# Splitting every weight chunk on VectorE, with ten pairs of places in the second part of a two-layer decoder trunk

## The chip, the core and the metric

The kernel runs on one core of a Trainium2 chip. The core has five engines that each work through their own list of instructions in order: TensorE (PE; its weight loads are shown apart as PEld), VectorE (DVE), ScalarE (ACT), GpSimd (POOL) and SyncE (SP, which here only issues DMA transfers). They wait for each other by semaphores. The metric is the device time of one execution in microseconds; lower is better.

## The reference

Two decoder layers over 256 tokens of width 1024, in float32. Cut to what matters here:

```python
for layer in range(2):
    h = rwkv_moba_mixer(x, ...) if layer == 0 else dilated_mixer(x, c_w_in, c_w_out, pos)
    x = layer_norm(2 ** 0.5 * x + h, ln1_g[layer], ln1_b[layer])
    m = square(relu(x @ mlp_w1[layer])) @ mlp_w2[layer]        # 1024 -> 4096 -> 1024
    x = layer_norm(2 ** 0.5 * x + m, ln2_g[layer], ln2_b[layer])

# the mixer of layer 0: z = x @ ab_w_in; eight RWKV-7 heads and four block-attention heads; y @ ab_w_out
# the mixer of layer 1: z = x @ c_w_in;  24 query heads in three window groups over 8 key/value heads; o @ c_w_out
```

## The kernel before

**The weights are one stream of 211 chunks** of 128x1024 float32 (512 KB each), in the order in which they are used: 0 to 26 for the projections of layer 0, 27 to 34 for its output projection, 35 to 98 for the MLP of layer 0, 99 to 102 for half of the values of layer 1, 103 to 134 for its queries and keys (four chunks a head), 135 to 138 for the other values, 139 to 146 for its output projection, 147 to 210 for the MLP of layer 1. A transfer brings each into one of the `raw` tiles (four in the first part, six in the second); SyncE issues it when the chunk that lay there before has been split.

**Splitting.** From chunk 17 on a chunk isn't multiplied as it is. ScalarE writes `hi`, the chunk rounded to the fast matmul type (L95), and then another engine writes `lo`, the rest: `lo = raw - hi` (L97). The activations are split alike (`xh` and `xl`, `yh` and `yl`, `hh` and `hl`; L240 on ScalarE and L241 on VectorE), and each product takes three matmuls: high by high, low by high and high by low. `Stream.split` decides who writes `lo`: VectorE, or GpSimd for the chunks that the tuple `ON_POOL` names. These are 34 (the end of the output projection of layer 0), 36 to 39 and 42 (the first chunks of the MLP of layer 0), 100, and 150, 151, 161, 164 and 169 (MLP of layer 1).

**Places.** A split chunk lies in a pair of places (`hi`, `lo`) of a ring. The ring has four pairs (`NW1`) until the output projection of layer 0, when `add_pairs` puts `NW2` more in front. From there on `cur["np"]` is the number of pairs and `cur["look"]` is that less two: when the matmuls of chunk i are written, the split of chunk i + look is written ahead of them. It takes the place of chunk i - 2, so ScalarE can write it as soon as TensorE is done with that one.

**The transitions.** `tail` runs the last chunks of a matrix product, first for the token half 0, then for the half 1. The layer norm of half 0 (class `LN`; L260 and L261 sum and take statistics, L271 to L273 the reciprocal root, with a power on GpSimd at L273, L285 and L286 apply it) is computed on VectorE while TensorE multiplies for half 1; TensorE then transposes the normed half (L297) into `xh` and `xl`, and `by_token` starts the next product with half 0 while VectorE norms half 1. In `rest`, `up` computes four more groups of the MLP with the weights stationary (L225), and `up_trans` brings the first group into the same layout (L388, L240, L241). The rotary embedding of layer 1 (`rope`) uses VectorE (L859, L862) and GpSimd (L861, L863).

**Order.** The code is written in program order; a scheduler with priorities turns it into one list for each engine, and so may put an instruction earlier or later than it is written. `tc.high_priority()` pulls the layer norm forward. The three transitions that the prediction speaks of are: the output projection of layer 0 into its MLP (about 166 to 212 us), that MLP into layer 1 (about 356 to 383 us), and the output projection of layer 1 into its MLP (about 532 to 580 us).

Of the kernel before, what the change touches and what calls it, by code (L numbers as in the profile page):

```python
# [37 lines left out]
NCHUNK = 211  # L38

UNSPLIT = 17  # L40
ON_POOL = (34, 36, 37, 38, 39, 42, 100, 150, 151, 161, 164, 169)


STATIONARY = [1] * 9 + [0] * 4 + [1] * 14 + [0] * 8
_MLP = [0] * 8 + [1] * 8 + [0] * 16 + ([1] * 8 + [0] * 8) * 2
STATIONARY += _MLP + [0] * 4 + [1] * 32 + [0] * 12 + _MLP
LINE, STAT_AT = 64, 56
NW1, NW2, NR, NR2 = 4, 4, 4, 2
NS4, NS2 = 13, 6
RIGHT = "right"  # L50
HS = 8 * (16 * P + 16)
# [75 lines left out]
def trunk(ctx: ExitStack, tc: tile.TileContext, w_all, x_nat, x_t, par_in, lora_in, gup2_in, ln_in,  # L127
# [80 lines left out]
    st.load(1 + NR)  # L208
    st.on_pool = set(ON_POOL)

# [1106 lines left out]
```

## Time and profile before

| | |
|---|---|
| runs | 742.39, 736.24 and 742.59 us; median 742.39 us |
| profiled execution | 736.11 us, of which its span is 734.0 us |
| PE busy | 702.7 us (96%) |
| DVE busy | 477.6 us (65%) |
| ACT busy | 333.8 us (45%) |
| POOL busy | 154.9 us (21%) |
| granted TensorE clock, mean | 0.977 |

Busy time counts an instruction from its start to its end, also while it is held up in between; so a row that takes longer than its like elsewhere is a sign of something beside it. PE's figure has little room in it, and what matters is where its 31 us of idle time and its stretches at a lower clock lie. The clock is given as a share of full speed: 1.00 stands for 2.4 GHz and 0.50 for 1.2 GHz.

### The profile page before, as it was taken

The numbers are of one execution on the slowest core, as the hardware profiler recorded it, in microseconds if no ns is written. First come the engines' busy times: TensorE is split into PE (matmuls) and PEld (weight loads), VectorE is DVE, ScalarE is ACT, GpSimd is POOL, SyncE is SP. The second block draws the span as 40 slices with busy tenths as digits, with TensorE's granted clock in tenths as the row PEclk, the third lists the DMA queues.
The fourth block names the chain that finished last, engine by engine and source line by source line (L and its number), as shares of the span: only waits on it lengthen the run. The fifth ranks groups of instructions, "written<-read, shape, count | busy, mean of one in ns | idle before, by whom it ended". The sixth has DMA issues, their size and how long they took to land. (4 is left out here: it accounts for less than half of the span.)

```text
span 734.0 us, 11556 instructions
## 1 busy us (share of the span) xinstructions
PE 702.7 (96%) x4572; PEld 626.6 (85%) x4572; DVE 477.6 (65%) x733; ACT 333.8 (45%) x485; POOL 154.9 (21%) x115
## 2 busy tenths in 40 slices
PE   8999989998999999999999899999999999999995
PEld 6867888996789889989879799997878898998985
DVE  3748983579786545546598767885497754464645
ACT  4712446253375435545155445554436453363520
POOL 3000032026200000000014867785131110000001
PEclk9999995999899999999999999999999999999998
DMA  8366362037674666565088533443537565655401
GB/s 308 130 188 187 118 179 78 29 128 275 200 260 147 204 194 199 183 199 192 31 286 295 165 116 118 142 152 107 174 106 254 168 211 184 198 197 175 144 1 58
DMA packets 40566, 122.61 MB, mean 167 GB/s; under 512 B 8128, under 2 KB 10816, under 8 KB 40384
## 3 DMA queue, kind: packets, MB, share of 16 engines
q1 hardware_dynamic: 37856, 119.94, 49.5%
q10 hardware_dynamic: 2656, 1.93, 0.9%
q8 instruction: 36, 0.59, 0.3%
q14 instruction: 18, 0.15, 0.1%
HBM read 119.49 MB, written 2.36 MB: 166 GB/s over the span
## 5 line engine op out<-in xcount | busy, mean ns | idle before, releaser
L97 DVE TENSOR_TENSOR lo<-raw,hi 128x1024 fp32r<-128x1024 f32 x182 | 237.7, 1310 | 137.0 <-ACT hi L95 135.3
L95 ACT CAST hi<-raw 128x1024 fp32r<-128x1024 f32 x194 | 202.1, 1049 | 198.3 <-PE bank L231 98.2
L225 PE MATMUL bank<-xh,hi 128*128 128x256 f32 x720 | 175.7, 284 | 0.0
L225 PE MATMUL bank<-xl,hi 128*128 128x256 f32 x720 | 173.8, 281 | 0.0
L225 PEld LDWEIGHTS bank<-xh,hi 128*128 128x128 f32 x720 | 136.2, 189 | 1.4 <-issue 0.7
L225 PEld LDWEIGHTS bank<-xl,hi 128*128 128x128 f32 x720 | 136.4, 189 | 0.5
L231 PE MATMUL bank<-hi,hl 128*128 128x512 f32 (+1 forms) x288 | 105.8, 368 | 1.9 <-DVE hl L241 1.9
L232 PE MATMUL bank<-lo,hh 128*128 128x512 f32 (+1 forms) x288 | 105.3, 366 | 0.0
L230 PE MATMUL bank<-hi,hh 128*128 128x512 f32 (+1 forms) x288 | 104.7, 367 | 0.3 <-ACT hh L240 0.3
L225 PE MATMUL bank<-xh,lo 128*128 128x256 f32 x720 | 100.3, 281 | 0.0
L225 PEld LDWEIGHTS bank<-xh,lo 128*128 128x128 f32 x720 | 91.5, 190 | 0.0
L273 POOL TENSOR_TENSOR rs<-rs,mhalf 128x1 f32<-128x1 f32 x8 | 7.7, 960 | 321.4 <-DVE rs L272 321.4
L861 POOL TENSOR_TENSOR qk<-qk,ropec 32x512 f32<-32x512 f32 x20 | 49.9, 2496 | 79.2 <-DVE sw L859 79.2
L231 PEld LDWEIGHTS bank<-hi,hl 128*128 128x128 f32 x288 | 54.3, 189 | 11.1 <-DVE hl L241 2.5
L230 PEld LDWEIGHTS bank<-hi,hh 128*128 128x128 f32 x288 | 54.2, 189 | 9.5 <-ACT hh L240 0.5
L232 PEld LDWEIGHTS bank<-lo,hh 128*128 128x128 f32 x288 | 54.2, 188 | 8.8
L217 PE MATMUL bank<-xst,raw 128*128 128x256 f32 x208 | 46.2, 381 | 1.2 <-DMA xst<-in_x_t_dram 1.2
L217 PEld LDWEIGHTS bank<-xst,raw 128*128 128x128 f32 x208 | 39.2, 190 | 8.3 <-DMA xst<-in_x_t_dram 2.4
L97 POOL TENSOR_TENSOR lo<-raw,hi 128x1024 fp32r<-128x1024 f32 x12 | 30.3, 2533 | 56.2 <-ACT hi L95 50.5
L232 PE MATMUL bank<-lo,xh 128*128 128x512 f32 x96 | 37.7, 393 | 0.6 <-DVE lo L97 0.5
L230 PE MATMUL bank<-hi,xh 128*128 128x512 f32 x96 | 38.1, 396 | 0.0
L231 PE MATMUL bank<-hi,xl 128*128 128x512 f32 x96 | 37.5, 391 | 0.1
(236 smaller groups left out, 896.5 us busy)
## 6 DMA issues: line engine op xcount, KB each, us to landing
raw<-in_w_all_dram SPq DMA_DIRECT2D x210, 512.0 KB, 3.5
g<-in_ln_dram SPq DMA_DIRECT2D x4, 512.0 KB, 5.5
b<-in_ln_dram SPq DMA_DIRECT2D x4, 512.0 KB, 6.2
dA<-abT ACTq DMA_DIRECT2D x2, 512.0 KB, 3.6
x<-in_x_nat_dram SPq DMA_DIRECT2D x1, 1024.0 KB, 4.8
dmask<-in_dmask_dram SPq DMA_DIRECT2D x1, 576.0 KB, 6.5
xst<-in_x_t_dram ACTq DMA_DIRECT2D x2, 256.0 KB, 5.6
xst<-in_x_t_dram SPq DMA_DIRECT2D x2, 256.0 KB, 5.7
```

Source lines behind the costliest of these rows:

```text
L95: self.nc.scalar.copy(hi[:, cols], r[:, cols])
L97: eng.tensor_tensor(lo[:, cols], r[:, cols], hi[:, cols].bitcast(F32), ALU.subtract)
L217: nc.tensor.matmul(ps, hl[:, k * P:(k + 1) * P], xraw(k), start=k == 0, stop=k == KT - 1)
L225: nc.tensor.matmul(ps, w[:, k * P:(k + 1) * P], a[:, k, :], start=n == 0, stop=n == 3 * KT - 1)
L230: nc.tensor.matmul(acc, ah, hi[:, cols], start=first, stop=False)
L231: nc.tensor.matmul(acc, al, hi[:, cols], start=False, stop=False)
L232: nc.tensor.matmul(acc, ah, lo[:, cols], start=False, stop=last)
L273: nc.gpsimd.tensor_tensor(rs, rs, mhalf, ALU.pow)
L861: nc.gpsimd.tensor_tensor(qk[0:32, :], qk[0:32, :], rc, MUL)
```

## The change

The list of chunks that GpSimd splits becomes empty, so VectorE writes `lo` for all of them, and the second part adds six pairs of places in place of four (ten in all in place of eight, and so a look-ahead of eight chunks in place of six).

```diff
@@ -38,14 +38,14 @@
 UNSPLIT = 17
-ON_POOL = (34, 36, 37, 38, 39, 42, 100, 150, 151, 161, 164, 169)
+ON_POOL = ()
@@
 LINE, STAT_AT = 64, 56
-NW1, NW2, NR, NR2 = 4, 4, 4, 2
+NW1, NW2, NR, NR2 = 4, 6, 4, 2
```

In the listings below a number behind a name tells one buffer from another; `lo_74`, `lo_68`, `lo_70` and `lo_72` are the places of the first part, and those from `lo_1386` on the added ones. On GpSimd, from the end of the output projection of layer 0 to the first rotation of layer 1, this is taken out:

```order
-L97 TENSOR_TENSOR lo_1390<-raw_65,hi_1389 128x1024
-L97 TENSOR_TENSOR lo_74<-raw_1393,hi_73 128x1024
-L97 TENSOR_TENSOR lo_68<-raw_1394,hi_67 128x1024
-L273 TENSOR_TENSOR rs<-rs,mhalf 128x1
-L97 TENSOR_TENSOR lo_70<-raw_63,hi_69 128x1024
-L97 TENSOR_TENSOR lo_72<-raw_64,hi_71 128x1024
-L97 TENSOR_TENSOR lo_1390<-raw_1393,hi_1389 128x1024
-L273 TENSOR_TENSOR rs<-rs,mhalf 128x1 x2
-L97 TENSOR_TENSOR lo_74<-raw_65,hi_73 128x1024
-L273 TENSOR_TENSOR rs<-rs,mhalf 128x1
+L273 TENSOR_TENSOR rs<-rs,mhalf 128x1 x4
```

The seven splits (34, 36 to 39, 42 and 100) are gone, and the four powers of the layer norms (L273) stand alone.

On VectorE, at the first transition, the layer norm of the token half 0 stood in a row before (`u`, `st`, `mv` and `rs` are its steps; the banks 79 and 82 hold the sums of half 0, bank 80 the first of half 1):

```order
L260 SCALAR_TENSOR_TENSOR u<-x,bank_79 128x512
L260 SCALAR_TENSOR_TENSOR u<-x,bank_82 128x512
L261 BN_STATS st<-u 128x6 x2
L271 BN_AGGR mv<-st 128x2
L272 TENSOR_SCALAR rs<-mv 128x1
L285 SCALAR_TENSOR_TENSOR u<-u,mv,g_1401 128x512 x2
L260 SCALAR_TENSOR_TENSOR u<-x,bank_80 128x512
L286 SCALAR_TENSOR_TENSOR x<-u,rs,b_1403 128x512
L261 BN_STATS st<-u 128x6
L286 SCALAR_TENSOR_TENSOR x<-u,rs,b_1403 128x512
```

Nothing stood between the statistics and the norm there but a first step of half 1. Now, at the same place:

```order
L97 TENSOR_TENSOR lo_1394<-raw_1397,hi_1393 128x1024
L260 SCALAR_TENSOR_TENSOR u<-x,bank_79 128x512
L260 SCALAR_TENSOR_TENSOR u<-x,bank_82 128x512
L261 BN_STATS st<-u 128x6 x2
L97 TENSOR_TENSOR lo_1396<-raw_1398,hi_1395 128x1024
L271 BN_AGGR mv<-st 128x2
L260 SCALAR_TENSOR_TENSOR u<-x,bank_80 128x512
L272 TENSOR_SCALAR rs<-mv 128x1
L285 SCALAR_TENSOR_TENSOR u<-u,mv,g_1405 128x512
L261 BN_STATS st<-u 128x6
L286 SCALAR_TENSOR_TENSOR x<-u,rs,b_1407 128x512
L285 SCALAR_TENSOR_TENSOR u<-u,mv,g_1405 128x512
```

The splits 36 (`lo_1394`) and 37 (`lo_1396`) now stand ahead of and inside the norm, as split 34 does a few rows earlier, and steps of half 1 come between those of half 0; six splits in a row (39 to 44) follow the norm of half 1.

On TensorE, where `by_token` goes over to the token half 1 in the same transition, the order before was (bank_82 receives the second transpose of half 1, banks 77 and 76 are the sums of half 1, `hi_1391` is chunk 35):

```order
L297 MATMUL bank_82<-ident,x 128x128 x4
L230 MATMUL bank_77<-hi_1391,xh 128x512
L231 MATMUL bank_77<-hi_1391,xl 128x512
L232 MATMUL bank_77<-lo_1392,xh 128x512
L230 MATMUL bank_76<-hi_1391,xh 128x512
```

Now:

```order
L297 MATMUL bank_82<-ident,x 128x128 x4
L230 MATMUL bank_77<-hi_1391,xh 128x512
L230 MATMUL bank_76<-hi_1391,xh 128x512
L225 MATMUL bank_81<-xh,hi_1387 128x256
L231 MATMUL bank_77<-hi_1391,xl 128x512
L232 MATMUL bank_77<-lo_1392,xh 128x512
```

The first matmul of the next product (L225, chunk 43) has moved in front of the pass over half 1; it reads `xh` of both halves.

## Rows read from the trace of the kernel before

**Rows 1.** The page: each engine's busy time, and GpSimd's splits.

```profile
PE 702.7 (96%) x4572; PEld 626.6 (85%) x4572; DVE 477.6 (65%) x733; ACT 333.8 (45%) x485; POOL 154.9 (21%) x115
...
L97 POOL TENSOR_TENSOR lo<-raw,hi 128x1024 fp32r<-128x1024 f32 x12 | 30.3, 2533 | 56.2 <-ACT hi L95 50.5
```

**Rows 2.** Who PE waited for: us in total, times, longest us.

```profile
PE bank L1119 <- POOL qk L863: 7.7, 4, 3.3
PE bank L297 <- DVE x L286: 5.9, 4, 3.6
...
PE bank L232 <- DVE lo L97: 0.5, 1, 0.5
```

**Rows 3.** Timeline of PE, first transition: start us, us, what [idle before].

```profile
178.85 0.39 PE L230 MATMUL bank<-hi,yh 128*128 128x512 f32 x1
179.08 0.39 PE L231 MATMUL bank<-hi,yl 128*128 128x512 f32 x1
183.05 1.12 PE L297 MATMUL bank<-ident,x 128*128 128x128 f32 x4 [3.58 <-DVE x L286]
...
188.88 0.41 PE L231 MATMUL bank<-hi,xl 128*128 128x512 f32 x1
```

**Rows 4.** Windows, first and third transition: busy us by engine, PEclk, DMA share, GB/s.

```profile
180.00:184.00 4.00, 0.95 (x5) 0.96 (x6) 4.00 (x5) 0.14 (x1) 4.00 (x2) 0.76 0.46 150
184.00:188.00 4.00, 3.62 (x11) 2.54 (x11) 3.50 (x3) 2.55 (x4) 1.23 (x1) 0.50 0.70 242
...
571.00:577.00 6.00, 4.21 (x27) 3.35 (x27) 4.95 (x8) 3.31 (x8) 2.39 (x1) 1.00 0.81 264
```

**Rows 5.** Timeline of DVE, first transition.

```profile
166.19 4.56 DVE L97 TENSOR_TENSOR lo<-raw,hi 128x1024 fp32r<-128x1024 f32 x2
...
176.69 3.54 DVE L285 SCALAR_TENSOR_TENSOR u<-u,mv,g 128x512 f32<-128x512 f32 x2
...
180.76 2.23 DVE L286 SCALAR_TENSOR_TENSOR x<-u,rs,b 128x512 f32<-128x512 f32 x1
182.92 0.68 DVE L261 BATCH_NORM_STATS2 st<-u 128x6 f32<-128x512 f32 x1
```

**Rows 6.** Timeline of POOL, first transition.

```profile
178.98 1.00 POOL L273 TENSOR_TENSOR rs<-rs,mhalf 128x1 f32<-128x1 f32 x1
179.95 5.27 POOL L97 TENSOR_TENSOR lo<-raw,hi 128x1024 fp32r<-128x1024 f32 x2
```

**Rows 7.** Timeline of DVE, second transition.

```profile
359.87 1.41 DVE L285 SCALAR_TENSOR_TENSOR u<-u,mv,g 128x512 f32<-128x512 f32 x2
361.19 1.41 DVE L286 SCALAR_TENSOR_TENSOR x<-u,rs,b 128x512 f32<-128x512 f32 x2
...
365.91 1.21 DVE L97 TENSOR_TENSOR lo<-raw,hi 128x1024 fp32r<-128x1024 f32 x1
367.51 2.97 DVE L97 TENSOR_TENSOR lo<-raw,hi 128x1024 fp32r<-128x1024 f32 x1 [0.39 <-ACT hi L95]
```

**Rows 8.** Timeline of PE: one row of the second transition, two of the third.

```profile
376.08 0.50 PE L232 MATMUL bank<-lo,xh 128*128 128x512 f32 x1 [0.48 <-DVE lo L97]
...
541.22 0.66 PE L297 MATMUL bank<-ident,x 128*128 128x128 f32 x4 [1.64 <-DVE x L286]
...
575.91 0.50 PE L231 MATMUL bank<-hi,hl 128*128 128x512 f32 x1 [1.52 <-DVE hl L241]
```

**Rows 9.** Timelines of DVE and of POOL, third transition.

```profile
538.68 2.48 DVE L286 SCALAR_TENSOR_TENSOR x<-u,rs,b 128x512 f32<-128x512 f32 x1
...
572.25 2.48 DVE L416 TENSOR_TENSOR s<-r 128x512 f32<-128x512 f32 x1 [0.84 <-ACT r L414]
...
538.24 5.18 POOL L97 TENSOR_TENSOR lo<-raw,hi 128x1024 fp32r<-128x1024 f32 x2 [1.60 <-ACT hi L95]
...
571.80 2.39 POOL L97 TENSOR_TENSOR lo<-raw,hi 128x1024 fp32r<-128x1024 f32 x1 [3.81 <-ACT hi L95]
```

**Rows 10.** Timeline of ACT, start of the pass over half 1, first transition.

```profile
199.54 1.30 ACT L381 ACTIVATE r<-bank 128x512 f32<-128x512 f32 x2
```

## The prediction

> **What bounds the kernel now.** I began with the page: TensorE is busy for 702.7 of 734.0 us [rows 1], so nothing that only speeds up another engine counts unless it ends a wait of TensorE or a stretch at its lower clock. The list of who PE waited for comes next [rows 2]. The reader is to see two things in it. The split itself is hardly ever late: 0.5 us in one wait, in all 734. What is late is the layer norm (5.9 us in 4 waits for `x`) and, in layer 1, the rotated queries and keys (7.7 us in 4 waits for GpSimd). Then I followed the waits for `x` back on the timelines. At the first transition PE stops for 3.58 us ahead of the transposes [rows 3], and the clock then granted is 0.50, the 1.2 GHz level, through 184 to 188 us [rows 4]. VectorE is busy all that time, but look at what with: two L285 take 3.54 us and the L286 at 180.76 takes 2.23 [rows 5] (the next L286 is alike, 2.2 us), where the same instructions a stage later take 1.41 us for two of either kind [rows 7]. What differs is GpSimd: exactly then it writes `lo` for four chunks, the last two in 5.27 us [rows 6]. Every VectorE row of these tables that is far too long stands beside a GpSimd split: the splits at 166.19 and 367.51, L286 at 538.68, L416 at 572.25 [rows 5, 7, 9]; the GpSimd rows beside the last two are there too [rows 9].
>
> **What the change moves, in all.** Twelve splits leave GpSimd (30.3 us of its time, 2.53 each [rows 1]) and come to VectorE at 1.21 us when nothing runs beside them [rows 7]: 14.5 us more work there. VectorE is busy for 477.6 us of 734 on the average, so the sum hangs on where the twelve stand, and that is at the three transitions, where VectorE's results are what PE waits for.
>
> **First transition (34, 36 to 39, 42).** Three of these (34, 36, 37) now stand on VectorE ahead of the second `x` of token half 0: 3 x 1.21 = 3.6 us, and a step of half 1 that has moved up, 0.7. Against that stand the stretches that go: 4.56 - 2.42 = 2.1 us for the two splits at 166.19, 3.54 - 1.41 = 2.1 for L285, 2 x (2.23 - 0.70) = 3.1 for the two L286: 7.3 us. GpSimd's power (1.00 us) stood behind splits, from 178.98 on [rows 6], and now waits for VectorE alone. Step by step I get the first half of `x` at 181.2 us (it was 183.0) and the second at 183.2, some 2.6 earlier than it was. PE's side: matmuls follow each other at 0.23 us [rows 3]; seven were left for half 1 at the stop, and they now run first, so PE is free at 179.3 + 7 x 0.23, or 180.9, nearly when the first half of `x` is there. Then it waits four times for a little, 2.4 us in all (0.3 for `x`, 0.8 for `xh`, 0.4 for the second `x`, 0.9 for `xl`), since those seven no longer hide anything, and it reaches the first low product of chunk 35 at 184.65 instead of 188.88 [rows 3], with one matmul more behind it: 4.45 us won, the stretch at 1.2 GHz included. Some comes back later. The L225 that has moved ahead of the pass over half 1 needs `xh` of the second transpose, which ScalarE writes behind two L381 (1.30 us [rows 10]): 0.2 + 1.3 + 0.6 = 2.1 us after the last matmul of half 0, while PE has 0.85 us to do: 1.25 lost. That leaves 3.2. Between the two, VectorE does splits 38 to 44 and the norm of half 1 at 1.15 to 1.2 us a split against PE's 6 x 0.227 = 1.36 us a chunk; 39 to 42 come out within 0.15 us of when they are wanted. I take 0.6 off for that: **2.6 us**. The bounds are 0.8 (the clock falls all the same, below) and 4.45 (nothing comes back).
>
> **Second transition (100).** GpSimd's split stretched one VectorE split to 2.97 us [rows 7]. Two more pairs put two splits (99, 100) ahead of the norm, so three remain in the gap, 3.6 us in place of 1.21 + 2.97 and a wait of 0.4; the norm of half 1 comes 0.9 us earlier. PE's wait of 0.48 for `lo` [rows 8] goes, and a little of what it then waits for `x` and `xl`: **0.65 us**, between 0 (if `xl`, which still stands behind two splits, is as late as it was) and 1.3 (the wait and all of the 0.9).
>
> **Third transition (150, 151; 161, 164).** Without the pair of splits at 538.24 the L286 at 538.68 takes 0.70 instead of 2.48 [rows 9], and the second `x` is ready at 539.4, ahead of PE. PE's 1.64 us of waiting there [rows 8] go; a VectorE split now stands ahead of `xl`, ends at 540.5, and fits beside PE's transposes and four remaining matmuls: **1.7 us**, at least 0.4 if it didn't. At 572.25 L416 shrinks from 2.48 to 0.7 but starts 0.7 us later behind a split (164) that GpSimd had done: `hl` comes 1.1 to 1.25 us earlier, and PE's wait of 1.52 [rows 8] falls by as much: **1.2 us**, bounds 0.3 and 1.5. Chunk 169 stood beside nothing: 0.
>
> **The two pairs as such.** In steady running they cost and bring nothing by the rows: a place is still that of the chunk two before the one on PE, so ScalarE's `hi` starts at the same point of PE's program, and in layer 1 VectorE's and ScalarE's orders within a head are the same as before, only for chunks two further on. So I leave the 7.7 us of waits for GpSimd's rotation as they are, with 2 us either way. The end of the kernel has no splits in it.
>
> **Two pages.** The rows give the stretches; beside them the Trainium skill, SBUF — State Buffer, section "Who interferes with whom", says that a VectorE instruction with two SBUF inputs and a GpSimd instruction that reads SBUF take turns whole, whichever is issued first: [rows 5, 6] agree: L286 takes 2.23 us where 0.70 would do, and L261, with one input, 0.68. The Trainium skill, Perfetto Trace Analysis, section "Optimizing Scalar/DVE Operations", speaks against this change: where VectorE is saturated, giving work to GpSimd may make sense (though it warns of the shared port). VectorE is at 4.00 of 4 us in 180 to 184 [rows 4]; by that rule the first rival below would be right.
>
> **The sum.** 2.6 + 0.65 + 1.7 + 1.2 = 6.15 us. The profiled execution took 736.11 (734.0 of span), so **730.0 us**. The median of the three runs, 742.39, lies 6.3 us above it and the lowest, 736.24, beside it; nothing in the trace tells why, and against the median the same gain would give 736.2. I take the base whose rows I added up.
>
> **Rivals.** *VectorE becomes the bound (slower).* The stretched rows might be stretched by themselves, or by something that stays. Then 3.6 + 0.7 us are simply added ahead of the second `x` at the first transition, 1.25 comes back there, one split (1.2) stands ahead of `xl` and one ahead of L416 at the third, and nothing is won: 8 us, 744. It decides for this if L285 and L286 at the first transition stay above 1.4 us each with GpSimd idle. For it: VectorE has no idle time there. Against: four different instructions are stretched, all beside GpSimd. 0.06. *The clock falls all the same.* The four small waits at the first transition make 2.4 us within 3.7; the 3.58 us of before were followed by 1.2 GHz. If these are too, about 2 us are lost on the next 4 us of work, and the first term is 0.8 or less: 732. PE's idle 1.8 us within 571 to 577, also in pieces, left it at 1.00 [rows 4]. 0.2. *What is won is given back in layer 1.* The waits for the rotation are made of ScalarE, VectorE and GpSimd waiting for each other in turn; another start of the first head can lengthen one. One more as long as the longest, 3.3 us [rows 2], with a fall of the clock behind it like that of [rows 4], costs some 4 to 5 us: 734.5. 0.15. *The deeper ring ends those waits:* 7.7 us and the clock behind them, 720. The unchanged order there speaks against it. 0.05. The forecast itself: 0.54.
>
> **Chances and range.** About 1% is what a measurement of this kernel can tell from no change. The forecast is a gain of 6.15 us, 0.8%; a third of its spread (4 to 9 us) lies above 1%, and the last rival lies there whole, the second and third mostly below. The three runs before lie 6.3 us apart, which can widen or hide a difference of this size. I put faster by over 1% at 0.43, within 1% at 0.5, slower at 0.07. The range is from 725, where the first two terms reach their upper bounds and layer 1 gives 2, to 738, a gain of 4 to 5 against the median shown.
>
> **What would show it.** GpSimd busy for about 125 us. VectorE's busy time nearly as before (14.5 us more splits, some 17 us less stretching); L285 and L286 at 0.7 us each in all four norms. At the first transition, no wait of PE over 1 us ahead of the transposes and no clock of 0.50 after it, but a wait of about 1.2 us at the L225 ahead of the pass over half 1. At the third, no wait for `x`, and one for `hl` below 0.6. The waits for GpSimd's rotation in layer 1 still at 6 to 9 us. I am wrong if PE waits for `lo` by more than 2 us in all, or if the rows of layer 1 have moved.

## The result, and the profile after

The changed kernel took 728.3 us (median of 728.07, 727.49, 732.9 and 728.53) beside 742.49 us for the kernel before on the same chip: a ratio of 0.9864, 95% interval 0.9818 to 0.991. That ratio is taken over the fast runs; the two medians alone would give 0.981, the two profiled executions 0.989. Its profiled execution took 728.07 us (span 726.2) beside 736.11 (734.0): 8.0 us less.

First the busy line of the changed kernel's page (busy time, share, instructions), which answers to [rows 1]:

```profile
PE 702.6 (97%) x4572; PEld 627.8 (86%) x4572; DVE 473.7 (65%) x745; ACT 333.7 (46%) x485; POOL 125.4 (17%) x103
```

And its list of waits of TensorE (total, times, longest), which answers to [rows 2]:

```profile
PE bank L1119 <- POOL qk L863: 6.7, 4, 3.3
PE bank L757 <- DMA Tall<-dT: 1.7, 1, 1.7
...
PE bank L231 <- DVE xl L241: 0.9, 2, 0.5
PE bank L231 <- DVE hl L241: 0.7, 2, 0.4
...
PE bank L230 <- ACT xh L240: 0.7, 1, 0.7
```

VectorE has twelve splits more and is busy for 3.9 us less. The waits for `x` (5.9 us in 4) and the one for `lo` are gone from the list; those for the rotation are there.

Next the timeline of the changed kernel at the first transition (start, duration, engine, instruction, wait ahead of it), for VectorE first; it answers to [rows 5].

```profile
168.65 2.35 DVE L97 TENSOR_TENSOR lo<-raw,hi 128x1024 fp32r<-128x1024 f32 x2
...
179.00 1.21 DVE L97 TENSOR_TENSOR lo<-raw,hi 128x1024 fp32r<-128x1024 f32 x1
...
180.86 0.74 DVE L285 SCALAR_TENSOR_TENSOR u<-u,mv,g 128x512 f32<-128x512 f32 x1
...
182.12 0.73 DVE L286 SCALAR_TENSOR_TENSOR x<-u,rs,b 128x512 f32<-128x512 f32 x1
182.77 0.75 DVE L285 SCALAR_TENSOR_TENSOR u<-u,mv,g 128x512 f32<-128x512 f32 x1
...
184.19 0.75 DVE L286 SCALAR_TENSOR_TENSOR x<-u,rs,b 128x512 f32<-128x512 f32 x1
```

GpSimd there has this row alone until 187, which answers to [rows 6]:

```profile
181.08 0.92 POOL L273 TENSOR_TENSOR rs<-rs,mhalf 128x1 f32<-128x1 f32 x1 [13.08 <-DVE rs L272]
```

And TensorE, which answers to [rows 3]:

```profile
183.38 0.60 PE L297 MATMUL bank<-ident,x 128*128 128x128 f32 x4
184.66 0.73 PE L230 MATMUL bank<-hi,xh 128*128 128x512 f32 x2 [0.67 <-ACT xh L240]
185.22 0.60 PE L297 MATMUL bank<-ident,x 128*128 128x128 f32 x4
186.18 0.50 PE L231 MATMUL bank<-hi,xl 128*128 128x512 f32 x1 [0.36 <-DVE xl L241]
186.52 0.39 PE L232 MATMUL bank<-lo,xh 128*128 128x512 f32 x1
...
198.12 0.28 PE L225 MATMUL bank<-xh,hi 128*128 128x256 f32 x1
```

Two splits take 2.35 us where they took 4.56, L285 0.75 where a pair took 3.54, L286 0.73 to 0.75 where it took 2.23. GpSimd's power waits for VectorE alone. TensorE begins the transposes (183.38) without a wait and stops twice for a little. The L225 at 198.12, of which the prediction expected 1.25 us of waiting, does not wait.

The windows of TensorE (length, busy time, clock granted) answer to [rows 4]: no 0.50 behind the transition.

```profile
180.00:184.00 4.00, 3.98 (x20) 1.00 0.40 144
184.00:188.00 4.00, 2.98 (x14) 1.00 0.00 0
```

And the second and third transitions on VectorE, which answer to [rows 7, 9]:

```profile
371.12 2.35 DVE L97 TENSOR_TENSOR lo<-raw,hi 128x1024 fp32r<-128x1024 f32 x2
373.39 1.28 DVE L241 TENSOR_TENSOR xl<-bank,xh 128x512 fp32r<-128x512 f32 x2
...
534.02 0.73 DVE L286 SCALAR_TENSOR_TENSOR x<-u,rs,b 128x512 f32<-128x512 f32 x1
...
566.08 0.68 DVE L416 TENSOR_TENSOR s<-r 128x512 f32<-128x512 f32 x1
```

TensorE's waits there answer to [rows 8]:

```profile
374.13 0.50 PE L231 MATMUL bank<-hi,xl 128*128 128x512 f32 x1 [0.54 <-DVE xl L241]
...
567.95 0.50 PE L231 MATMUL bank<-hi,hl 128*128 128x512 f32 x1 [0.36 <-DVE hl L241]
```

L286 takes 0.73 (it was 2.48), L416 0.68 (2.48); the wait for `hl` is 0.36 (1.52), and at the second transition a wait of 0.54 for `xl` stands in place of that for `lo`.

**Where the time went, by stretches.** All traces are cut at the same five instructions, with the same number of matmuls between them (to one):

- *start*: from 0 to VectorE's second L842 (165.58 us before, 168.04 after), the part that the change doesn't touch;
- *first*: from there to the start of the last L225 row of the first token-wise pass of layer 0's MLP (216.08 and 213.29);
- then the MLP of layer 0, the same in both (129.52 us), to its last L225 row (345.60 and 342.81);
- *second*: from there, through the second transition and layer 1's attention, to the L260 of the third transition (532.58 and 527.92);
- *third*: from there to the L225 pass behind `up_trans` (577.84 and 569.88).

Each figure below is a difference of two starts on the timeline; the ratio is to the kernel before in the same session, with its interval. Rows of a kernel that was run twice are two traces.

| kernel | start | first | second | third | median us | ratio |
|---|---|---|---|---|---|---|
| before | 165.58 | 50.50 | 186.98 | 45.26 | 742.49 | |
| before, again | 165.91 | 50.62 | 184.10 | 45.25 | 737.76 | 0.9999 (0.9959 to 1.0039) |
| after | 168.04 | 45.25 | 185.11 | 41.96 | 728.3 | 0.9864 (0.9818 to 0.991) |
| after, again | 165.94 | 45.23 | 184.96 | 41.94 | 727.93 | 0.9865 (0.9804 to 0.9927) |
| no GpSimd splits, 8 pairs | 167.05 | 45.21 | 184.85 | 41.95 | 727.1 | 0.9831 (0.9772 to 0.989) |
| GpSimd splits, 10 pairs | 165.56 | 51.41 | 188.43 | 42.13 | 734.35 | 0.9947 (0.9908 to 0.9987) |
| first six splits moved | 164.72 | 45.18 | 185.75 | 45.28 | 729.73 | 0.9905 (0.9865 to 0.9945) |
| GpSimd repeats 12 differences | 164.93 | 55.50 | 188.26 | 50.25 | 750.4 | 1.0158 (1.0091 to 1.0225) |
| GpSimd fills a tile 12 times | 165.83 | 46.97 | 189.60 | 41.96 | 729.78 | 0.9869 (0.9813 to 0.9924) |
| rotations on VectorE | 155.24 | 46.97 | 183.39 | 41.94 | 715.09 | 0.9691 (0.964 to 0.9742) |
| sum of the rotation on VectorE | 157.85 | 45.19 | 191.71 | 41.96 | 724.03 | 0.9807 (0.9755 to 0.9859) |
| rotations of the first part only | 155.19 | 47.27 | 185.04 | 41.94 | 717.2 | 0.9755 (0.9688 to 0.9821) |
| before, with rotations on VectorE | 157.13 | 51.56 | 185.57 | 46.85 | 728.34 | 0.9878 (0.9823 to 0.9934) |
| rotations and sums on VectorE | 156.22 | 47.27 | 177.58 | 41.99 | 709.38 | 0.9635 (0.9586 to 0.9685) |

From before to after: -5.25 in the first stretch, -1.87 in the second, -3.30 in the third, +2.46 at the start and +0.16 behind the third: -7.80 us, the difference of the spans. Of the second, 0.88 had been won by the same point of layer 1's first L225 pass (384.92 before, 381.25 after, less the 2.79 won until 345.60), the rest in the attention.

### The profile page after: what moved, and what is told of

Its sections match the earlier page's. It is cut to its first block, busy times and chain, and to the rows that moved or that the text cites. A ratio compares the mean times of both kernels' runs of the same rounds, so it can differ in the third digit from the quotient of the medians.

```text
span 726.2 us, 11562 instructions
## 1 busy us (share of the span) xinstructions
PE 702.6 (97%) x4572; PEld 627.8 (86%) x4572; DVE 473.7 (65%) x745; ACT 333.7 (46%) x485; POOL 125.4 (17%) x103
## 4 chain that ended last, share of the span: by engine, by line
PE 78%; DVE 10%; POOL 3%; ACT 3%; issue 2%; DMA 2%; POOLq 0%; SPq 0%; DVEq 0%; ACTq 0%
PE bank L225 24%; PE bank L231 13%; PE bank L232 13%; PE bank L230 13%; PE bank L217 5%; DVE lo L97 3%; POOL qk L861 2%; PE bank L732 2%; ACT hi L95 1%; POOL qk L863 1%; PE bank L1121 1%; DVE sw L859 1%; DVE e L866 1%; DVE gI L684 1%; DVE gtmp L682 1%
## 5 line engine op out<-in xcount | busy, mean ns | idle before, releaser
L97 DVE TENSOR_TENSOR lo<-raw,hi 128x1024 fp32r<-128x1024 f32 x194 | 244.6, 1269 | 135.5 <-ACT hi L95 133.8
L225 PE MATMUL bank<-xh,hi 128*128 128x256 f32 x720 | 176.2, 284 | 0.0
L225 PE MATMUL bank<-xl,hi 128*128 128x256 f32 x720 | 174.4, 281 | 0.0
L225 PEld LDWEIGHTS bank<-xh,hi 128*128 128x128 f32 x720 | 136.4, 190 | 1.5 <-issue 0.7
L225 PEld LDWEIGHTS bank<-xl,hi 128*128 128x128 f32 x720 | 136.8, 190 | 0.4
L231 PE MATMUL bank<-hi,hl 128*128 128x512 f32 (+1 forms) x288 | 105.8, 368 | 0.7 <-DVE hl L241 0.7
L225 PE MATMUL bank<-xh,lo 128*128 128x256 f32 x720 | 100.5, 281 | 0.0
L225 PEld LDWEIGHTS bank<-xh,lo 128*128 128x128 f32 x720 | 91.8, 190 | 0.0
L273 POOL TENSOR_TENSOR rs<-rs,mhalf 128x1 f32<-128x1 f32 x8 | 7.0, 880 | 399.2 <-DVE rs L272 399.2
L861 POOL TENSOR_TENSOR qk<-qk,ropec 32x512 f32<-32x512 f32 x20 | 53.7, 2685 | 77.4 <-DVE sw L859 77.4
L231 PEld LDWEIGHTS bank<-hi,hl 128*128 128x128 f32 x288 | 54.3, 189 | 9.8 <-DVE hl L241 1.4
L217 PE MATMUL bank<-xst,raw 128*128 128x256 f32 x208 | 47.7, 390 | 0.7 <-DMA xst<-in_x_t_dram 0.7
L217 PEld LDWEIGHTS bank<-xst,raw 128*128 128x128 f32 x208 | 40.7, 196 | 7.9 <-DMA xst<-in_x_t_dram 1.4
L231 PE MATMUL bank<-hi,xl 128*128 128x512 f32 x96 | 37.7, 393 | 0.9 <-DVE xl L241 0.9
L863 POOL TENSOR_TENSOR qk<-qk,sw 32x512 f32<-32x512 f32 x20 | 31.9, 1594 | 3.7 <-DVE mx L893 1.6
```

Of the source, the lines that this page charges most:

```text
L97: eng.tensor_tensor(lo[:, cols], r[:, cols], hi[:, cols].bitcast(F32), ALU.subtract)
L217: nc.tensor.matmul(ps, hl[:, k * P:(k + 1) * P], xraw(k), start=k == 0, stop=k == KT - 1)
L225: nc.tensor.matmul(ps, w[:, k * P:(k + 1) * P], a[:, k, :], start=n == 0, stop=n == 3 * KT - 1)
L231: nc.tensor.matmul(acc, al, hi[:, cols], start=False, stop=False)
L861: nc.gpsimd.tensor_tensor(qk[0:32, :], qk[0:32, :], rc, MUL)
L863: nc.gpsimd.tensor_tensor(qk[0:32, :], qk[0:32, :], sw, ADD)
```

## Experiments

**The two halves of the change apart.** First the splits alone:

```diff
 # the changed kernel
-NW1, NW2, NR, NR2 = 4, 6, 4, 2
+NW1, NW2, NR, NR2 = 4, 4, 4, 2
```

> The splits alone: none on GpSimd, eight pairs of places as before. Three stretches are measured, each free of the first part. First transition, from VectorE's second L842 to the last L225 of the first token-wise pass of layer 0's MLP: 50.50 us before, 45.25 after. Second transition and attention, from the last L225 of layer 0's MLP to the layer norm (L260) of layer 1's MLP: 186.98 and 185.11. Third, from that L260 to the first L225 of the second token-wise pass: 45.26 and 41.96. Theory 1 (GpSimd's splits held VectorE and the power up; the pairs bring nothing): 45 to 46.5, 185 to 186.5, 42 to 42.5, in all within 2 us of the changed kernel. Theory 2 (the gain comes from the two pairs, which put three splits ahead of the norm): 49 to 50.5, 187, 44 to 45.3, a time like that of the kernel before. Theory 3 (both are needed: VectorE with all splits but without the head start is late at the first transition): more than 50.5 in the first stretch.

All three stretches came out as after the whole change, within 0.3 us, and so did the time. Then the pairs alone:

```diff
 # the kernel before
-NW1, NW2, NR, NR2 = 4, 4, 4, 2
+NW1, NW2, NR, NR2 = 4, 6, 4, 2
```

> The two pairs alone: ten pairs of places in the second part, the twelve splits on GpSimd as before. Theory 1 (GpSimd's splits are the cause): first stretch 49 to 51 us (50.50 before, 45.25 after the whole change), third 44.5 to 46 (45.26, 41.96), second within 1.5 of 187; the time within 2 us of the kernel before. Theory 2 (the pairs are the cause): 45 to 47 and 42 to 43, and a time like that of the changed kernel. L285 and L286 at the first transition: above 1.4 us each by theory 1.

The first stretch went as theory 1 has it (51.41), the third did not: 42.13, nearly all of the gain there, with GpSimd splitting. The time is 0.53% under that of the kernel before, its interval clear of 1 (0.9908 to 0.9987), a little more than the 2 us I allowed. The timeline of this kernel shows why, first VectorE at the first transition and, in the last row, at the third:

```profile
176.67 5.64 DVE L285 SCALAR_TENSOR_TENSOR u<-u,mv,g 128x512 f32<-128x512 f32 x2
...
182.82 2.74 DVE L286 SCALAR_TENSOR_TENSOR x<-u,rs,b 128x512 f32<-128x512 f32 x1
...
541.16 0.74 DVE L286 SCALAR_TENSOR_TENSOR x<-u,rs,b 128x512 f32<-128x512 f32 x1
```

And GpSimd, ahead of the second transition in the first row and ahead of the third in the others:

```profile
347.96 2.39 POOL L97 TENSOR_TENSOR lo<-raw,hi 128x1024 fp32r<-128x1024 f32 x1 [152.59 <-ACT hi L95]
...
526.03 2.38 POOL L97 TENSOR_TENSOR lo<-raw,hi 128x1024 fp32r<-128x1024 f32 x1 [2.86 <-ACT hi L95]
529.12 2.40 POOL L97 TENSOR_TENSOR lo<-raw,hi 128x1024 fp32r<-128x1024 f32 x1 [0.70 <-ACT hi L95]
```

With two more chunks of look-ahead GpSimd's two splits are over at 531.5, ahead of the norm (535 to 542), and L286 takes 0.74 us. At the first transition they stay beside it, and L285 takes 2.8 us each. The second transition is the same: split 100 runs at 347.96 in place of 366.61, ahead of the norm (358 to 363), and from the last L225 row of layer 0's MLP to the same row of layer 1's first L225 pass it is 38.44 us, as after the whole change (39.32 before). The second stretch as a whole hides that, because the attention behind it took 149.99 us (147.66 before). So what costs is that the two engines read at the same time, not who splits. Each half of the change can give the gain of the second transition (0.9 us) and nearly all of the third's (3.1 of 3.3); both together give no more than one.

**One transition alone.**

```diff
 # the kernel before
-ON_POOL = (34, 36, 37, 38, 39, 42, 100, 150, 151, 161, 164, 169)
+ON_POOL = (100, 150, 151, 161, 164, 169)
```

> The first transition alone: of the twelve splits the six of the first transition (34, 36 to 39, 42) go to VectorE, the six later ones (100, 150, 151, 161, 164, 169) stay on GpSimd; eight pairs of places. If the places act each for itself: first stretch 45.2 us as with all twelve gone (50.50 before), third 45.3 as before (42.0 with all gone), second 185 to 189. If instead the splits at the third transition were late because of what stood earlier in the program, the third stretch shrinks too. The time by this lies between the two kernels, about 5 us under the kernel before.

45.18 and 45.28, as said: the places act each for itself. The time fell by more than the 5 us that I gave (729.73 beside 738.65 us): in the trace the start (0.86 us earlier) and the attention (1.23) went its way too, and neither is shown to be the splits'.

**The contention put back.** GpSimd does twelve instructions again, in the kernel of the first experiment, and no engine uses what they write; the instructions of VectorE, ScalarE and TensorE and their order are the same in the three.

```diff
 # the changed kernel with NW2 = 4; spare is a tile of its own
+AGAIN = (34, 36, 37, 38, 39, 42, 100, 150, 151, 161, 164, 169)
 ...
         eng.tensor_tensor(lo[:, cols], r[:, cols], hi[:, cols].bitcast(F32), ALU.subtract)
+        if i in AGAIN:    # first kernel: the difference once more
+            self.nc.gpsimd.tensor_tensor(self.spare, r[:, cols], hi[:, cols].bitcast(F32), ALU.subtract)
+        if i in AGAIN:    # second kernel: one column, then a fill
+            self.nc.gpsimd.tensor_copy(self.spare[:, 0:1], hi[:, 0:1].bitcast(F32))
+            self.nc.gpsimd.memset(self.spare, 0.0)
```

> As the kernel with the splits alone (none on GpSimd, eight pairs), and GpSimd computes the same twelve differences once more into a tile that nobody reads. VectorE, ScalarE and TensorE have the same instructions in the same order; nothing waits for GpSimd's result. Theory 1 (two engines with two operands in SBUF hold each other up): VectorE's L285, L286 and splits beside it are stretched again, to 1.5 to 2.9 us instead of 0.7 and 1.2; since VectorE now has twelve more splits than in the kernel before, the first stretch is 50 to 56 us, longer than before (50.50), the third 44 to 46.5. Theory 2 (it only mattered who makes lo, or in which order): 45 to 46.5 and 42 to 42.5 as with the splits alone. Theory 3 (only GpSimd's queue mattered: the power L273 behind the splits): between, with L285 and L286 at 0.7 but a later L273.

> As the one before, but at the same twelve places GpSimd copies one column of hi and then fills a tile of 128x2560 with zeros (by the 0.95 us of a 128x1024 fill some 2.2 us), so it is as busy and its queue as long, and reads next to nothing. Theory 1 (the operands that both read): L285 and L286 stay at 0.7 us, the splits at 1.2; only the power L273 can come late behind the fills, so the first stretch is 45 to 48 us, the third 42 to 43.5. Theory 3 (GpSimd's queue, with the power in it, was the cause): both as with the repeated differences, 49 us and more.

The timeline with the repeated differences, VectorE:

```profile
179.95 2.17 DVE L288 SCALAR_TENSOR_TENSOR u<-u,mv,g 128x512 f32<-128x512 f32 x1
182.04 0.68 DVE L264 BATCH_NORM_STATS2 st<-u 128x6 f32<-128x512 f32 x1
182.65 2.73 DVE L289 SCALAR_TENSOR_TENSOR x<-u,rs,b 128x512 f32<-128x512 f32 x1
185.31 2.84 DVE L288 SCALAR_TENSOR_TENSOR u<-u,mv,g 128x512 f32<-128x512 f32 x1
...
188.66 2.48 DVE L289 SCALAR_TENSOR_TENSOR x<-u,rs,b 128x512 f32<-128x512 f32 x1
```

GpSimd beside it:

```profile
182.50 5.09 POOL L100 TENSOR_TENSOR spare<-raw,hi 128x1024 f32<-128x1024 f32 x2
```

The timeline with the fills, VectorE:

```profile
176.80 1.21 DVE L98 TENSOR_TENSOR lo<-raw,hi 128x1024 fp32r<-128x1024 f32 x1
...
178.66 0.75 DVE L289 SCALAR_TENSOR_TENSOR u<-u,mv,g 128x512 f32<-128x512 f32 x1
...
180.91 0.75 DVE L290 SCALAR_TENSOR_TENSOR x<-u,rs,b 128x512 f32<-128x512 f32 x1 [0.90 <-POOL rs L277]
```

GpSimd beside it:

```profile
176.89 1.16 POOL L100 COPY spare<-hi 128x1 f32<-128x1 f32 x1
178.11 2.26 POOL L101 MEMSET spare<- 128x2560 f32 x1
180.31 0.56 POOL L277 TENSOR_TENSOR rs<-rs,mhalf 128x1 f32<-128x1 f32 x1
```

(The added lines shift the numbers: L288 and L289, or L289 and L290, are L285 and L286.) GpSimd is as busy in both, 159.5 and 159.6 us by their pages. Where it reads two operands, L285 and L286 take 2.2 to 2.8 us, the first stretch is 55.50 (+10.3), the third 50.25 (+8.3), and the kernel is slower than the one before. Where it fills, they take 0.75; only the power comes 0.9 us late behind a fill, and the first stretch is 46.97 (+1.8), the third unchanged. Theory 1 holds, and theory 3 (the queue) explains 1.8 of 10.3 us. One thing does hang on the repeated differences: a `raw` tile is free for the next load only when GpSimd has read it too, and SyncE waits for that 9.0 us in all, four times. It is not what TensorE waits for: its waits of 4.21 and 2.75 us at the first transition are for `x`, and ScalarE's waits for loads are no longer than without the differences (14.1 and 15.7 us). The third stretch went further than the 46.5 us I allowed: `x`, `xl` and `hl` are late one after the other there, by 1.66, 1.89 and 3.12 us.

**Is layer 1's part of the gain the change's?** The changed kernel and the kernel before ran once more, unchanged.

> The changed kernel once more, for a second trace and beside the others on one chip. If layer 1's attention goes one of two ways by chance, the second stretch (185.11 us in the first trace) may come out at 188 to 190 here, with waits of PE for the rotation like those of the kernel before (2.8 us ahead of the sixth head); if its way is fixed by the order of the instructions, it is 184.8 to 185.4 again and the single waits (3.3, 1.2, 1.2, 1.1 us) come back at the same heads. First and third stretch: 45.2 and 42.0 within 0.3.

> The kernel before once more, against itself. If layer 1's way is fixed by the program, the second stretch is 186.5 to 187.5 again (186.98), with the longest waits for the rotation ahead of the first and the sixth head (3.3 and 2.8 us), and part of the changed kernel's gain there (1.9 us) belongs to the change. If the way is taken by chance, from the length of the first stretch at 1.2 GHz in the attention, it can come out at 185 or at 189. First and third stretch: 50.5 and 45.3 within 0.3. The ratio to itself: 1 within about 1%.

After: the same again (184.96). Before: 184.10 us where the first trace had 186.98, with waits for the rotation of 2.8, 1.2, 1.2 and 1.1 us, like those of the changed kernel. One program goes either way, so the 1 us that the attention seemed to give is not shown to be the change's. What parts the ways is seen behind the first of those waits. TensorE's windows (stretch, length, busy, clock) in the first trace after:

```profile
416.00:418.00 2.00, 2.00 (x7) 0.50 0.78 221
418.00:420.00 2.00, 2.00 (x12) 0.75 0.09 37
420.00:422.00 2.00, 2.00 (x20) 1.00 0.00 0
```

In the kernel with the fills:

```profile
416.00:418.00 2.00, 2.00 (x7) 0.50 0.42 162
418.00:420.00 2.00, 2.00 (x9) 0.50 0.00 0
420.00:422.00 2.00, 2.00 (x15) 0.72 0.00 0
```

And in the kernel before, again:

```profile
418.00:420.00 2.00, 0.14 (x1) 1.00 0.77 246
420.00:422.00 2.00, 2.00 (x13) 1.00 0.67 215
```

After a wait of 3.27, 2.76 and 2.78 us the clock is at the 1.2 GHz level until about 419, until about 421, and not at all. The kernel with the fills then waits 2.81 us once more ahead of a later head, where after waits 1.07. That the fall decides the way fits these traces; it wasn't tried by itself.

**The next step: GpSimd's other work.** By the same theory the rotation (L861 and L863 on GpSimd) should go to VectorE too.

```diff
 # the changed kernel, in rope
-        nc.gpsimd.tensor_tensor(qk[0:32, :], qk[0:32, :], rc, MUL)
+        nc.vector.tensor_tensor(qk[0:32, :], qk[0:32, :], rc, MUL)
         nc.vector.tensor_tensor(sw, sw, rs_, MUL)
-        nc.gpsimd.tensor_tensor(qk[0:32, :], qk[0:32, :], sw, ADD)
+        nc.vector.tensor_tensor(qk[0:32, :], qk[0:32, :], sw, ADD)
```

> A try at the next step: on top of the changed kernel the two products and sums of the rotation (L861, L863) are computed by VectorE in place of GpSimd, where 32x512 takes VectorE about 0.68 us (L862) and GpSimd 1.25 to 4.07. Theory 1 goes on: GpSimd and VectorE hold each other up in layer 1 too; PE's waits for the rotation (6.7 us in 4) fall below 2, VectorE's splits there go back from 2.2 to 1.2 us, the second stretch is 180 to 184 us (185.11 in the changed kernel) and the time 722 to 727. Rival: VectorE is busy for 69 of the 90 us from 410 to 500, and 16 to 18 rotations at 1.36 bring 22 to 24 more; it is full, PE waits for its scores or splits instead, and the second stretch is 187 us or more.

> Half of that: L861 (the product) stays on GpSimd, L863 (the sum, which PE waits for) goes to VectorE behind L862. Theory 1: the chain ends a GpSimd row of 1.25 to 2.72 us earlier, but GpSimd's product still stands beside VectorE's splits and stretches them; waits 2 to 5 us, second stretch 183 to 186. Rival: VectorE, waiting in order for GpSimd's product, is held up itself and its splits behind the sum come late: 187 or more.

Both rows moved: 715.09 us, better than either theory had for the time; the second stretch (183.39) and the waits are as theory 1 has them. The 40 rows took GpSimd 85.6 us (53.7 and 31.9) and take VectorE 28.1 (14.6 and 13.5); the waits for the rotation fall from 6.7 to 0.8 us, but new ones of 4.2 us come for the sums of the probabilities, so the second stretch is only 1.7 shorter. The larger part, 10 to 13 us, came at the start. With only the sum (L863) moved, the second stretch is 191.71: VectorE waits in its order for GpSimd's product (20.1 us in 18 waits), as the rival said, and TensorE's waits for the rotation are 7.5 us in place of 6.7; the time, 724.03, is lower all the same, by the start.

```diff
 # the changed kernel: rotations of the first part only
+        eng = nc.vector if pool is pa else nc.gpsimd
-        nc.gpsimd.tensor_tensor(qk[0:32, :], qk[0:32, :], rc, MUL)
+        eng.tensor_tensor(qk[0:32, :], qk[0:32, :], rc, MUL)
         nc.vector.tensor_tensor(sw, sw, rs_, MUL)
-        nc.gpsimd.tensor_tensor(qk[0:32, :], qk[0:32, :], sw, ADD)
+        eng.tensor_tensor(qk[0:32, :], qk[0:32, :], sw, ADD)
```

> Where the rotation's move brought its 12 us: on top of the changed kernel only the two rotations of the first part go to VectorE, the 18 of layer 1 stay on GpSimd. Theory 1 (the first part's gain is the stretch at 1.2 GHz around 110 to 135 us, which follows waits that GpSimd's rotation takes part in): VectorE's second L842 at 155 to 158 us in place of 164 to 168, no granted clock of 0.50 ahead of it, second stretch 185 as in the changed kernel, time 716 to 719. Rival (the whole chain of rotations in layer 1 is the gain): L842 at 165 or later and a time of 725 or more.

(The trace has four rotations in the first part and 16 in layer 1, not two and 18.) 717.2 us, with the start at 155.19. The clock line of the page after, in 40 slices:

```profile
PEclk9999995899999999999999999999999999999999
```

That of this kernel:

```profile
PEclk9999999999999999999999999999999999999998
```

The stretch at 1.2 GHz around 110 to 132 us is gone, and with it the wait for `Tall` (1.7 us) ahead of it. The scheduler also wrote another order there, so the rotation itself and that order are not told apart. The first stretch is 47.27 here, 2.0 us longer than after: TensorE waits 0.37, 0.68 and 0.39 us for `x`, `xh` and `xl`, and then the clock falls. The window of this kernel (all engines' busy time, clock, DMA):

```profile
174.00:176.00 2.00, 2.00 (x8) 1.60 (x8) 2.00 (x4) 0.02 (x1) 0.99 (x1) 0.50 0.00 0
```

With all rotations on VectorE the same three waits come, and a fourth and fifth (0.51 and 0.22 us) where half 1 comes, but the clock stays at 1.00: 46.97.

```diff
 # the kernel before, with the rotations on VectorE as above
 ON_POOL = (34, 36, 37, 38, 39, 42, 100, 150, 151, 161, 164, 169)
```

> The rotation's move without the change: the kernel before (twelve splits on GpSimd, eight pairs) with all rotations on VectorE. If the two edits add up: L842 at 155 to 158 us, first and third stretches as before the change (50 to 51 and 45 us), the second 183 to 186, the time 723 to 727. If the change only brought what the rotation's move brings too: 715 to 718.

Against the same with the change (46.97, 183.39, 41.94) it has 51.56, 185.57 and 46.85: the change is worth 4.6 and 4.9 us in the first and third there as well. The time (728.34) and both stretches are above what I gave. In the third, 1.6 us are the clock's: behind the same wait of 1.52 us for `hl` it is 0.50 from 568 to 570 us here, and stayed at 1.00 in the kernel before [rows 4], so the change's own part of the 4.9 is 3.3 as before. The two edits add up: the ratios 0.9878 and 0.9864 multiply to 0.974, and both together gave 0.9691 (0.964 to 0.9742).

```diff
 # the changed kernel with all rotations on VectorE; in d_scores
-            nc.gpsimd.tensor_tensor(dd, e[:, o:o + n], e[:, o + n:o + 2 * n], ADD)
-            nc.gpsimd.tensor_tensor(dd, dd, e[:, o + 2 * n:o + 3 * n], ADD)
+            nc.vector.tensor_tensor(dd, e[:, o:o + n], e[:, o + n:o + 2 * n], ADD)
+            nc.vector.tensor_tensor(dd, dd, e[:, o + 2 * n:o + 3 * n], ADD)
```

> One step beyond the rotation's move: L1132 and L1133, the sums of the probabilities over the query heads, go to VectorE too, so that GpSimd has almost nothing left in layer 1. PE's waits for the scaled sums (4.2 us in 3 with the rotation moved) should fall below 2 if GpSimd's adds are what is late there: second stretch 181 to 183 (183.4), time 712 to 715. Rival: VectorE's order is now full, its splits and scores come later: 185 or more.

709.38 us, the fastest here, 3.65% under the kernel before, and a second stretch of 177.58: both better than I gave. The page's busy line:

```profile
PE 691.4 (98%) x4572; PEld 617.9 (87%) x4572; DVE 486.1 (69%) x817; ACT 332.6 (47%) x485; POOL 21.4 (3%) x31
```

The list of TensorE's waits, its two longest:

```profile
PE bank L217 <- DMA xst<-in_x_t_dram: 1.5, 2, 1.1
PE bank L1141 <- ACT pp L1134: 1.4, 2, 1.0
```

GpSimd has lost 104.0 us of work against the changed kernel, and VectorE has gained 12.4.

## Why the prediction was right, and where it was off

**The cause** held: four kinds of VectorE rows were too long because of GpSimd beside them, and shrank as said. The repeated differences bring the long rows back, the fills do not. The Trainium skill, SBUF — State Buffer, section "Who interferes with whom", which the prediction weighed, has this case as it came out (two operands in SBUF against a GpSimd instruction that reads); the one-input L264 (L261 of the kernel before) between them stays at 0.68 us.

**First transition: 2.6 predicted, 5.25 measured**, above the upper bound of 4.45. At the first low product of chunk 35 (L231) the gain was 5.16 by the start times (188.88 and 186.18, less the 2.46 of the start), and 5.39 with the one matmul more behind it, where I had 4.45. So 0.94 us lie in the four small waits, which I put at 2.4 us: the first half of `x` was ready 0.8 us sooner than I had stepped out, and two waits came, 0.67 and 0.36. The larger step that failed is what I took back: 1.25 us at the moved L225, and 0.6 for tight splits. That L225 reads only the first part of `xh`, written at 196.03 ahead of the two L381, not the second behind them; it started at 198.12 without a wait, and no wait for `lo` came. Only 0.14 us were given back by the end of the stretch.

**Second transition: 0.65 predicted, 0.88 measured**, within 0 to 1.3; `xl` behind two splits is a little late, as the lower bound had it (0.54 us).

**Third transition: 1.7 and 1.2 predicted, 2.16 and 1.14 measured** (from L260 to the first token-wise pass 33.23 us before and 31.07 after, by the L225 at 565.81 and 558.99; the rest of the stretch behind it). No wait for `x`, one of 0.36 for `hl`. What I did not see is that the two pairs would give nearly all of both (2.20 and 0.93 in the kernel with the pairs alone) without moving a split.

**The two pairs: 0 predicted.** With the splits moved they bring nothing that the stretches show (within 0.3 us). By themselves they bring 0.9 us at the second transition and 3.1 at the third, because the longer look-ahead lets GpSimd split ahead of the norms. My reason for the 0 (the same point of TensorE's program in steady running) left the transitions out, where the order of the splits changes.

**Layer 1: 0 within 2 predicted, 1 us measured**, and the kernel before differs by 2.9 us from itself there.

**The start: not in the sum.** It came 2.46 us later in the first trace after (0.36 in the second), by a longer stretch at 1.2 GHz (until about 132 us, before until about 127), in instructions that the change leaves alone. So the time met the forecast (728.3 for 730.0) because a term that was 2.65 us too small and a loss that has nothing to do with the change stood against each other. Free of start and attention the change is worth 5.25 + 0.88 + 2.16 + 1.14 = 9.4 us, 1.3%, in place of the 6.15 I added up. With that sum I held a change within 1% for likelier (0.5) than a gain above it (0.43); the measured gain, 1.36% with an interval from 0.9 to 1.8%, is most likely on the other side.

**The rivals.** VectorE did not become the bound: L285 and L286 fell to 0.75 us, far below the 1.4 that decided for it. The clock did not fall behind the first transition in either trace of the changed kernel (two waits, 1.03 us in all). That rival was nearer than this shows: in two of the kernels that also carry the moved rotations it did, behind three waits of 1.4 us in all, and in a third it didn't behind the same three. The deeper ring left the waits for the rotation where they were (6.7 us). The rule of the Trainium skill, Perfetto Trace Analysis, section "Optimizing Scalar/DVE Operations", that a saturated VectorE may hand work to GpSimd, goes the other way in every run here: each piece of work taken from GpSimd, splits, rotations and sums, made the kernel faster (for the rotations of the first part, together with another order); only in the second stretch did the half of the rotation cost time, where VectorE waited for GpSimd inside its own order. The page's own reservation on the shared port is what holds.

## What to carry to other kernels

Where an instruction takes two or three times as long as its like elsewhere, look what GpSimd does in that microsecond; a second engine that reads the same memory may not be a second engine at all. Cost a move from GpSimd to VectorE not by its own duration but by the stretched rows on both sides: 104.0 us on GpSimd became 12.4 us more on VectorE here. The order alone can do it too: with two more pairs the same splits stood on GpSimd ahead of the norms of the second and third transitions, and the gain came there without moving any. And before a wait is put on a moved instruction, check which part of the tile it reads: here the half that was written first.

## What the hardware showed that I had not expected

- GpSimd's copy of one column took 1.16 us beside a VectorE split, and ended with it (178.05 and 178.01); the twelve copies took from 0.18 to 1.17 us. A fill of 128x2560 took 2.24 us on the mean, and no VectorE row beside one was longer than its like; only the power behind one in GpSimd's own queue came late.
- The clock's fall is not a function of the program: a wait of 2.8 us was followed by the 1.2 GHz level for some microseconds, or not at all. At the start it came in every trace of the kernels before and after, between 110 and 132 us; in the kernels with the rotation there on VectorE (or its sum alone) it came in none, and their start is 8 to 13 us shorter. How much of that is the clock, and how much the other order, is not shown.
- The spread of the times went with it: the kernel before ran from 732.36 us at a mean granted clock of 0.986 to 743.34 at 0.969 on one chip, the kernel with the rotations on VectorE from 714.92 to 716.48, all four runs at 0.994.
